# Modulation of a two-layer trunk: 32 of 48 column blocks as VectorE products with rows of the transposed weights

## The chip, the cores and the metric

The kernel runs on one core of one Trainium2 chip. A time is the device time of one execution in microseconds. The median of the runs of the kernel before is 5885.44 us (5885.08 to 5893.9, three runs). One further execution was profiled, and all rows come from it.

## The reference

A trunk of two layers works on 512 latent tokens x and 256 context tokens, 1024 wide, in float32. Each layer has a token mixer (four branches: pooling, a state space scan, a gated delta rule scan with a triangular inverse, a Fourier transform; each is weighted by gates and merged) and a retrieval of experts. Both are modulated: the shift, the scale and the gate of each of the two sub-layers are column blocks of one product of a conditioning vector with a matrix of 1024 x 6144.

```python
silu_c = jax.nn.silu(c)
silu_cc = jax.nn.silu(c_ctx)[None]
for l in range(DEPTH):
    mod_x = jnp.split(silu_c @ w_mod[l] + b_mod[l], 6, axis=-1)
    mod_c = jnp.split(silu_cc @ w_mod[l] + b_mod[l], 6, axis=-1)
    h_c = _modulate(ctx, mod_c[0], mod_c[1])
    if l == DEPTH - 1:
        states = context_states(h_c, lp, zero_states)
    else:
        mix_c, states = token_mixer(h_c, lp, zero_states, None)
        ctx = _layer_norm(DEEPNORM_ALPHA * ctx + mod_c[2][:, None] * mix_c, ...)
        ...
    h_x = _modulate(x, mod_x[0], mod_x[1])
    mix_x, _ = token_mixer(h_x, lp, states, rows)
    x = _layer_norm(DEEPNORM_ALPHA * x + mod_x[2][:, None] * mix_x, ...)
    ...
```

In the last layer the context is needed for the states of the scans alone, so only shift and scale (the first 16 column blocks of 128) of the context's modulation are used there; x uses all 48 blocks in both layers.

## The kernel before

`run` goes through the layers. A layer's mixer has two stages. In m1 the context is normalised and sent through the scans (`recurrent`); in m2 x goes through them, from the context's states. In layer 0's m2 the gather of experts for the context runs beside it: GpSimd gathers rows (`gat<-in_u`) and VectorE takes their dot products with a row `hb`, by a scalar_tensor_tensor of 128x1024 with an accumulated output (`gat<-gat,hb`).

A weight block is loaded as 128x512 in float32 (256 KB, tile `wraw`, or `xwraw` in the second lane, x), split into a high part (`xwhi`, ScalarE) and a low part (`xwlo`, VectorE), and multiplied on TensorE in three matmuls for each 128 columns. One unit of `gates` for the context takes four such loads, so 48 matmuls of 256 columns, then two tanh on ScalarE and two stores `gd<-xs` on SyncE's queue. A unit of gates for x has matmuls of 512 columns.

The modulation comes from `mod_steps`: for each of 12 groups of 512 columns, eight loads of 256 KB and eight matmuls with a result of 2x512 (both streams at once: x and context), a copy to SBUF, four small transposes and an addition of the bias into `modfm`. These matmuls take float32 operands as they are, and each shows as two instructions in the trace (`ps<-wraw,sc` in the first lane, `pa<-xwraw,sc` in the second). Layer 0's groups 0 to 3 (shift and scale of the first sub-layer) are made at the very start by `mod`, since the norm of the context waits for them. Groups 4 to 11 are the first filler of the second lane in layer 0's m1, ahead of the gates. All 12 groups of layer 1 are a filler added after layer 0's `mix_out`, with a low priority; in the scheduled program they stand in layer 0's m2, beside the scans of x and the gather.

Fillers are generators whose steps are called at points that a table (FC, FX) gives between the steps of the scans; over that a list scheduler decides the order of the instructions on each engine, once, when the program is built. Engines then work through their instructions in that order. DMA loads are issued by SyncE in such an order too. The tile `hb` (128x1024, `x4()`) has two buffers. The buffer `hx` holds the normalised x, transposed, in layer 0's m1.

All recorded instructions have the line of one helper, L145 (L155 in the kernel after).

## Time and profile before

| | us |
|---|---|
| median of three runs (lowest, highest) | 5885.44 (5885.08, 5893.9) |
| the profiled execution | 5897.45 |
| its span in the trace | 5895.7 |
| TensorE busy | 5041.2 (86%) |
| VectorE busy | 4232.6 (72%) |
| ScalarE busy | 1939.1 (33%) |
| GpSimd busy | 1862.3 (32%) |

The profile names engines PE (TensorE matmul), PEld (its weight loads), DVE (VectorE), ACT (ScalarE), POOL (GpSimd) and SP (SyncE, which issues loads and stores). Busy time of PE is a sum over pipelined matmuls, whose single durations overlap, so the pace of a row of matmuls is read from the starts. The chain of waits that the page gives covers the last part of the span alone, not the stages that the change touches; these are read by windows. The stages at hand are these: 0 to 66 us, the start up to the first four groups; 66 to 276, the context's projections and the modulation's other eight groups, up to the first row of the triangular inverse of the first stage; 276 to 545, the rest of the context's mixer; 1200 to 1420, layer 1's modulation in layer 0's m2; 3505 to 3663 and 3663 to 3800, layer 1's m1 before and after its inverse begins.

### The profile page before, as it was taken

The numbers are of one execution on the slowest core, as the hardware profiler recorded it, in microseconds if no ns is written. First come the engines' busy times: TensorE is split into PE (matmuls) and PEld (weight loads), VectorE is DVE, ScalarE is ACT, GpSimd is POOL, SyncE is SP. The second block draws the span as 40 slices with busy tenths as digits, with TensorE's granted clock in tenths as the row PEclk, the third lists the DMA queues.
The fourth block names the chain that finished last, engine by engine and source line by source line (L and its number), as shares of the span: only waits on it lengthen the run. The fifth ranks groups of instructions, "written<-read, shape, count | busy, mean of one in ns | idle before, by whom it ended". The sixth has DMA issues, their size and how long they took to land. (4 is left out here: it accounts for less than half of the span.)

```text
span 5895.7 us, 76828 instructions
## 1 busy us (share of the span) xinstructions
PE 5041.2 (86%) x26902; PEld 4234.5 (72%) x26902; DVE 4232.6 (72%) x7951; ACT 1939.1 (33%) x3519; POOL 1862.3 (32%) x1338
## 2 busy tenths in 40 slices
PE   8998977987568777799889879999888989988888
PEld 3887755843457677799667768787777989977766
DVE  4656287787888889788777786457565567877777
ACT  2444321321023322244323354333234323433333
POOL 0001544224553775544333310000003443433332
PEclk9999998998678888899999999999998989999999
DMA  6556469788887774999899954433434348998996
GB/s 214 177 164 194 143 227 312 245 259 315 275 278 266 241 245 150 315 350 346 315 326 345 328 197 136 124 113 111 135 125 133 126 142 282 350 331 325 327 335 242
DMA packets 613556, 1410.10 MB, mean 239 GB/s; under 512 B 97968, under 2 KB 221488, under 8 KB 613168
## 3 DMA queue, kind: packets, MB, share of 16 engines
q1 hardware_dynamic: 465712, 868.26, 43.8%
q0 software_dynamic: 147456, 536.94, 26.7%
q8 instruction: 211, 3.46, 0.2%
q14 instruction: 177, 1.45, 0.1%
HBM read 1244.52 MB, written 160.43 MB: 238 GB/s over the span
## 5 line engine op out<-in xcount | busy, mean ns | idle before, releaser
L145 POOL DMA_INDIRECT gat<-in_u,gidx x512 | 686.1, 1340 | 1038.2 <-DVE gat L145 959.9
L145 POOL DMA_INDIRECT gat<-in_v,gidx x512 | 651.3, 1272 | 906.1 <-DVE gacc L145 776.4
L145 DVE SCALAR_TENSOR_TENSOR gacc<-gat,gact,gacc 128x1024 f32<-128x1024 f32 x508 | 692.2, 1363 | 117.7 <-DMA gat<-in_v,gidx 112.8
L145 PE MATMUL ps<-hx 128*128 128x512 f32 x3072 | 752.7, 394 | 0.0
L145 DVE SCALAR_TENSOR_TENSOR gat<-gat,hb 128x1024 f32<-128x1024 f32 x512 | 617.6, 1219 | 108.5 <-DMA gat<-in_u,gidx 106.9
L145 PEld LDWEIGHTS ps<-hx 128*128 128x128 f32 x3072 | 588.5, 192 | 125.4
L145 PE MATMUL ps<-hx,dh 128*128 128x384 f32 x2304 | 601.8, 342 | 1.4 <-ACT dh L145 1.4
L145 PE MATMUL pa<-hx 128*128 128x512 f32 x1536 | 419.8, 408 | 170.7 <-ACT hx L145 157.8
L145 PE MATMUL ps<-s,s 128*128 128x128 f32 (+3 forms) x2752 | 420.3, 310 | 151.8 <-issue 83.9
L145 PEld LDWEIGHTS ps<-s,s 128*128 128x128 f32 (+1 forms) x2752 | 375.4, 213 | 225.3 <-issue 119.6
L145 ACT CAST dh<-du 128x1024 fp32r<-128x1024 f32 x256 | 268.6, 1051 | 785.5 <-PE ps L145 417.9
L145 PE MATMUL pa<-hx,dh 128*128 128x384 f32 x1792 | 511.3, 355 | 9.2 <-ACT da L145 7.4
L145 PEld LDWEIGHTS pa<-hx 128*128 128x128 f32 x1536 | 295.5, 196 | 248.9 <-ACT hx L145 164.6
L145 PEld LDWEIGHTS ps<-hx,dh 128*128 128x128 f32 x2304 | 422.0, 191 | 3.3 <-ACT dh L145 3.3
L145 PE MATMUL ps<-hx,dl 128*128 128x384 f32 x1152 | 393.3, 342 | 31.2 <-DVE dl L145 31.2
L145 PE MATMUL ps<-hx,whi 128*128 128x512 f32 x1152 | 386.9, 404 | 16.5 <-ACT whi L145 16.5
L145 DVE TENSOR_TENSOR hx<-dv,hx 128x1024 fp32r<-128x1024 f32 x256 | 313.0, 1223 | 119.0 <-ACT hx L145 115.1
L145 ACT CAST xwhi<-xwraw 128x512 fp32r<-128x512 f32 x352 | 218.2, 620 | 530.9 <-PE pa L145 418.8
L145 PE MATMUL pa<-hx,xwhi 128*128 128x512 f32 x1152 | 382.5, 406 | 8.0 <-DVE ld L145 3.6
L145 PE MATMUL pa<-hx,dl 128*128 128x384 f32 x896 | 322.8, 360 | 67.9 <-POOL dl L145 57.2
L145 ACT CAST hx<-dv 128x1024 fp32r<-128x1024 f32 x256 | 268.5, 1049 | 292.0 <-PE ps L145 175.7
L145 ACT CAST whi<-wraw 128x512 fp32r<-128x512 f32 x320 | 197.8, 620 | 490.6 <-PE ps L145 282.5
(283 smaller groups left out, 10177.9 us busy)
## 6 DMA issues: line engine op xcount, KB each, us to landing
du<-in_ut SPq DMA_DIRECT2D x256, 512.0 KB
dv<-in_v SPq DMA_DIRECT2D x256, 512.0 KB
xwraw<-in_w_in SPq DMA_DIRECT2D x272, 256.0 KB
acts<-da SPq DMA_DIRECT2D x256, 192.0 KB
a<-acts SPq DMA_DIRECT2D x256, 192.0 KB
wraw<-in_w_in SPq DMA_DIRECT2D x176, 256.0 KB
xwraw<-in_w_mod SPq DMA_DIRECT2D x160, 256.0 KB
rest<-wst SPq DMA_DIRECT2D x48, 768.0 KB
```

The source lines that it names most:

```text
L145: r = f(*a, **kw)
```

## The change

Groups 0 to 3 stay as they are. Column blocks 16 to 47 (groups 4 to 11) of both layers are computed by a new generator, `mod_rows`: for each block it loads 128 rows of the transposed weights (128x1024, 512 KB, into `hb`) and makes for each stream one scalar_tensor_tensor on VectorE, 128x1024, whose accumulated output is the dot product of each row with silu of the conditioning vector, which is broadcast over the partitions. The sum goes straight to its column of `modfm`. At the end the bias is added, once for all.

- Layer 0: both streams, so 64 products. They are no longer a filler of their own: `gates` for the context calls the generator twice after each of its 16 units (`beside`). The broadcast rows and the scratch output lie in three slices of the buffer that later becomes `hx`, so the norm of x (`norm_late`) allocates `hx` after that.
- Layer 1: x alone, 32 products, in layer 1's own m1, beside `gatesx`, with the row in the tile `gacc`. In layer 0's m2 four of the 12 groups stay.

```diff
+    def mod_rows(self, l, fm, streams, tiles):
+        nc, io = self.nc, self.io
+        n0 = 16
+        rows = []
+        for s in streams:
+            row = tiles[s]
+            nc.sync.dma_start(row, io["cr"][s:s + 1, :].to_broadcast([128, 1024]))
+            th = self.x4()
+            nc.scalar.activation(th, row, AF.Tanh, scale=0.5)
+            nc.vector.scalar_tensor_tensor(row, th, 1.0, row, op0=OP.add, op1=OP.mult)
+            rows.append(row)
+        for n in range(n0, 48):
+            w = self.x4()
+            nc.sync.dma_start(w, io["w_modt"][l, n - n0])
+            for i, s in enumerate(streams):
+                out = w if i == len(streams) - 1 else tiles[2]
+                nc.vector.scalar_tensor_tensor(out, w, 0.5, rows[i], op0=OP.mult, op1=OP.mult,
+                                               accum_out=fm[:, n, s:s + 1])
...
+            yield
...
-    def gates(self, l, h, T, gd, branches=range(4)):
+    def gates(self, l, h, T, gd, branches=range(4), beside=None):
...
                 self.proj_fm(self.io["w_in"][l], U_GATE + 4 * b + u, h, T, fn)
+                if beside is not None:
+                    for _ in range(2):
+                        next(beside, None)
                 yield
...
-                        self.add(self.mod_steps(l, range(4, 12), fm))
-                        gates = self.add(self.gates(l, hc, 256, mc[0]))
+                        free = [free[:, 1024 * i:1024 * i + 1024] for i in range(3)]
+                        gates = self.add(self.gates(l, hc, 256, mc[0], beside=self.mod_rows(l, fm, (0, 1), free)))
...
-                    gatesx = self.add(self.gates(l, hx, 512, mx[0], range(4 if last else 2)))
+                    self.add(self.norm_late(x, fm, hx))
+                    hx = hx.parts
+                    gatesx = self.add(self.gates(l, hx, 512, mx[0], range(4 if last else 2),
+                                                  self.mod_rows(l, fm, (0,), [self.keep([128, 1024], "gacc", 1)]) if last else None))
...
-                        self.add(self.mod_steps(l + 1, range(12), fm1))
+                        self.add(self.mod_steps(l + 1, range(4), fm1))
```

The order of instructions differs at three places. The first is VectorE in layer 0's m1, where the context's convolutions begin (`ps,vec` is a convolution's product, `wlo` and `xwlo` are low parts of split weights, `modfm` is the modulation). Before:

```order
L145 SCALAR_TENSOR_TENSOR s_221_622<-s_222_628,s_221_622 128x256
L145 SCALAR_TENSOR_TENSOR s_237_705<-ps_631,vec_6_75,s_237_705 128x254
L145 TENSOR_TENSOR wlo_782<-wraw_779,whi_781 128x512
L145 SCALAR_TENSOR_TENSOR s_237_705<-ps_631,vec_6_75,s_237_705 128x255 x2
L145 TENSOR_TENSOR wlo_820<-wraw_817,whi_819 128x512
L145 SCALAR_TENSOR_TENSOR s_237_705<-ps_631,vec_6_75,s_237_705 128x254
L145 TENSOR_TENSOR wlo_838<-wraw_835,whi_837 128x512
L145 SCALAR_TENSOR_TENSOR s_237_705<-s_238_711,s_237_705 128x256
L145 SCALAR_TENSOR_TENSOR s_239_714<-ps_632,vec_6_75,s_239_714 128x254
L145 TENSOR_TENSOR wlo_856<-wraw_853,whi_855 128x512
```

After (`hb` holds rows of the transposed weights, `hx` the broadcast rows and the scratch):

```order
L155 SCALAR_TENSOR_TENSOR hb_1282,modfm_179<-hb_1282,hx_131 128x1024
L155 SCALAR_TENSOR_TENSOR hx_131,modfm_179<-hb_1286,hx_131 128x1024
L155 TENSOR_TENSOR xwlo_1295<-xwraw_1292,xwhi_1294 128x512
L155 TENSOR_TENSOR wlo_698<-wraw_695,whi_697 128x512
L155 SCALAR_TENSOR_TENSOR hb_1286,modfm_179<-hb_1286,hx_131 128x1024
L155 TENSOR_TENSOR wlo_716<-wraw_713,whi_715 128x512
L155 TENSOR_TENSOR xwlo_1313<-xwraw_1310,xwhi_1312 128x512
L155 TENSOR_TENSOR wlo_754<-wraw_751,whi_753 128x512
L155 SCALAR_TENSOR_TENSOR hx_131,modfm_179<-hb_1370,hx_131 128x1024
L155 SCALAR_TENSOR_TENSOR s_235_731<-ps_657,vec_6_75,s_235_731 128x254
L155 TENSOR_TENSOR wlo_772<-wraw_769,whi_771 128x512
```

Products with the transposed rows, two to a load, and low parts of the gates' weights stand between the convolutions. Up to the inverse's first row VectorE has 27 `xwlo` splits before and 73 after, and all 64 products; all 16 gate units of the context stand ahead of the inverse, where 6 did. On SyncE's queue the 21 `xwraw` loads that lay among the first 32 `wraw` loads of the modulation at the start give way to 8 `xwraw` loads of the projection and two broadcast rows.

The second place is TensorE in layer 0's m2, at the state space scan of x (`s`, `masks`), with layer 1's modulation (`xwraw,sc`). Before:

```order
L145 MATMUL pa_15959<-xwraw_15963,sc_185 2x512
L145 MATMUL ps_11653<-s_2754_11651,s_2751_11644 128x256 x2
L145 MATMUL pa_15959<-xwraw_15966,sc_185 2x512
L145 MATMUL pa_15959<-xwraw_15969,sc_185 2x512
L145 MATMUL pa_15959<-xwraw_15972,sc_185 2x512
L145 MATMUL ps_11662<-s_2758_11660,masks_66 128x512
L145 MATMUL pa_15959<-xwraw_15975,sc_185 2x512
L145 MATMUL pa_15959<-xwraw_15978,sc_185 2x512
L145 MATMUL pa_15959<-xwraw_15981,sc_185 2x512
L145 MATMUL ps_11669<-s_2761_11667,masks_66 128x512
```

After, the last of the four groups that stay, and the scan behind it:

```order
L155 MATMUL ps_11128<-s_2588_11126,s_2585_11119 128x256 x2
L155 MATMUL pa_15699<-xwraw_15721,sc_185 2x512
L155 MATMUL ps_11137<-s_2592_11135,masks_66 128x512
L155 MATMUL pa_15726<-masks_66,xs_3804_15724 128x2 x4
L155 MATMUL ps_11144<-s_2595_11142,masks_66 128x512
L155 MATMUL ps_11153<-s_2599_11151,s_2585_11119 128x256 x2
L155 MATMUL ps_11162<-s_2603_11160,masks_66 128x512
L155 MATMUL ps_11169<-s_2606_11167,masks_66 128x512
L155 MATMUL ps_11174<-s_2587_11124,s_2594_11139 128x64
```

The eight later groups no longer stand between the scan's matmuls.

The third place is VectorE in layer 1's m1, at the context's convolutions. Before:

```order
L145 TENSOR_TENSOR xwlo_29880<-xwraw_29877,xwhi_29879 128x512
L145 SCALAR_TENSOR_TENSOR s_6235_29520<-s_6236_29526,s_6235_29520 128x256
L145 SCALAR_TENSOR_TENSOR s_6237_29529<-ps_29447,vec_8_80,s_6237_29529 128x254
L145 SCALAR_TENSOR_TENSOR s_6237_29529<-ps_29447,vec_8_80,s_6237_29529 128x255 x2
L145 SCALAR_TENSOR_TENSOR s_6237_29529<-ps_29447,vec_8_80,s_6237_29529 128x254
L145 TENSOR_TENSOR xwlo_29898<-xwraw_29895,xwhi_29897 128x512
L145 SCALAR_TENSOR_TENSOR s_6237_29529<-s_6238_29535,s_6237_29529 128x256
```

After:

```order
L155 SCALAR_TENSOR_TENSOR s_6084_29061<-ps_28979,vec_8_80,s_6084_29061 128x254
L155 SCALAR_TENSOR_TENSOR hb_30391,modfm_393<-hb_30391,gacc_27778 128x1024
L155 SCALAR_TENSOR_TENSOR s_6084_29061<-ps_28979,vec_8_80,s_6084_29061 128x255
L155 TENSOR_TENSOR wlo_29111<-wraw_29108,whi_29110 128x512
L155 SCALAR_TENSOR_TENSOR s_6084_29061<-ps_28979,vec_8_80,s_6084_29061 128x255
L155 TENSOR_TENSOR wlo_29129<-wraw_29126,whi_29128 128x512
L155 SCALAR_TENSOR_TENSOR s_6084_29061<-ps_28979,vec_8_80,s_6084_29061 128x254
L155 TENSOR_TENSOR xwlo_29759<-xwraw_29756,xwhi_29758 128x512
L155 SCALAR_TENSOR_TENSOR s_6084_29061<-s_6085_29067,s_6084_29061 128x256
L155 SCALAR_TENSOR_TENSOR s_6100_29144<-ps_29070,vec_8_80,s_6100_29144 128x254
L155 SCALAR_TENSOR_TENSOR hb_30548,modfm_393<-hb_30548,gacc_27778 128x1024
```

Products with x's row (`gacc`) stand between the convolution's steps, two to a gate unit. Up to the inverse's first row there are 32 `xwlo` splits where there were 24, so two gate units of 512 columns have moved ahead of it, and all 32 products stand there too. GpSimd's order is the same in both kernels.

## Rows read from the trace of the kernel before

**Rows 1.** The page, part 1: busy us (share of the span) xinstructions of each engine.

```profile
...
PE 5041.2 (86%) x26902; PEld 4234.5 (72%) x26902; DVE 4232.6 (72%) x7951; ACT 1939.1 (33%) x3519; POOL 1862.3 (32%) x1338
```

**Rows 2.** Windows: length, busy us of each engine, granted TensorE clock, DMA share, GB/s.

```profile
...
0.00:66.00 66.00, 51.10 (x129) 9.25 (x129) 7.49 (x23) 6.26 (x12) 1.29 (x6) 1.00 0.82 258
66.00:276.00 210.00, 196.41 (x1204) 146.54 (x1204) 135.34 (x285) 88.45 (x182) 3.76 (x2) 0.95 0.55 173
276.00:545.00 269.00, 238.36 (x1744) 220.00 (x1744) 165.07 (x336) 114.83 (x243) 7.09 (x6) 0.94 0.60 181
1000.00:1100.00 100.00, 94.36 (x409) 77.16 (x408) 89.19 (x159) 31.82 (x53) 41.46 (x35) 0.97 0.83 274
1305.00:1420.00 115.00, 100.07 (x334) 35.85 (x333) 88.05 (x158) 17.01 (x30) 49.77 (x41) 0.93 0.90 318
1420.00:1600.00 180.00, 90.93 (x457) 81.11 (x457) 139.28 (x232) 15.13 (x28) 92.64 (x78) 0.64 0.84 285
3505.00:3663.00 158.00, 148.06 (x859) 125.95 (x858) 104.45 (x214) 77.81 (x160) 4.93 (x4) 0.97 0.42 127
3663.00:3800.00 137.00, 133.83 (x725) 106.59 (x724) 68.87 (x158) 39.91 (x72) 0.00 (x0) 1.00 0.44 137
```

**Rows 3.** Waits of VectorE, 66 to 276 us: us in total, times, longest us.

```profile
...
DVE wlo L145 <- ACT whi L145: 18.9, 22, 3.7
DVE s L145 <- PE ps L145: 13.2, 12, 4.1
```

**Rows 4.** Groups of TensorE, 0 to 66 us: busy us, mean ns, idle before.

```profile
...
L145 PE MATMUL ps<-wraw,sc 128*2 128x512 f32 x64 | 33.3, 627 | 14.9 <-DMA wraw<-in_w_mod 14.6
L145 PE MATMUL pa<-xwraw,sc 128*2 128x512 f32 x40 | 20.3, 592 | 0.0
```

**Rows 5.** Timeline of TensorE near 131 us: start, length, instruction, count.

```profile
...
131.24 6.25 PE L145 MATMUL pa<-xwraw,sc 128*2 128x512 f32 x14
```

**Rows 6.** Groups of TensorE, 66 to 276 us.

```profile
...
L145 PE MATMUL pa<-xwraw,sc 128*2 128x512 f32 x88 | 41.9, 601 | 0.1
```

**Rows 7.** Timeline of VectorE: products with accumulate, back to back.

```profile
...
1296.21 1.22 DVE L145 SCALAR_TENSOR_TENSOR gat<-gat,hb 128x1024 f32<-128x1024 f32 x1
1297.36 0.08 DVE L145 DVE_READ_ACCUMULATOR gat<-gat,hb 128x1 f32 x1
...
1298.50 0.08 DVE L145 DVE_READ_ACCUMULATOR gat<-gat,hb 128x1 f32 x1
```

**Rows 8.** Timeline of SyncE: gate stores, two to a unit of 256 columns.

```profile
...
287.14 0.33 SPq L145 DMA_DIRECT2D gd<-xs  x1
...
293.07 0.33 SPq L145 DMA_DIRECT2D gd<-xs  x1
```

**Rows 9.** Groups of VectorE, 66 to 276 us.

```profile
...
L145 DVE TENSOR_TENSOR xwlo<-xwraw,xwhi 128x512 fp32r<-128x512 f32 x27 | 18.4, 687 | 10.2 <-ACT xwhi L145 9.1 <-DMA gd<-xs 1.2
```

**Rows 10.** Timeline of VectorE: first row of layer 0's first inverse.

```profile
...
276.12 2.11 DVE L145 TENSOR_TENSOR gat<-gat,gat 64x31 f32<-64x31 f32 x8 [1.81 <-DMA gat<-in_eye]
```

**Rows 11.** Waits of TensorE, 276 to 545 us.

```profile
...
PE pa L145 <- DVE ld L145: 13.1, 6, 5.9
```

**Rows 12.** Groups of TensorE, 1305 to 1420 us.

```profile
...
L145 PE MATMUL pa<-xwraw,sc 128*2 128x512 f32 x114 | 58.2, 628 | 9.8 <-DMA xwraw<-in_w_mod 9.8
...
L145 PE MATMUL pa<-masks,xs 2*128 2x2 f32 x32 | 3.4, 208 | 2.8 <-ACT xs L145 2.8
```

**Rows 13.** Waits of VectorE, 1305 to 1420 us.

```profile
...
DVE gat L145 <- DMA gat<-in_u,gidx: 9.7, 8, 2.4
```

**Rows 14.** Timeline of TensorE: matmuls of 512 columns.

```profile
...
3700.17 0.61 PE L145 MATMUL pa<-hx,xwhi 128*128 128x512 f32 x2
3700.63 0.39 PE L145 MATMUL pa<-hx,xwlo 128*128 128x512 f32 x1
```

**Rows 15.** Timeline of all engines: a 512 KB load and its reader.

```profile
...
596.10 1.53 SPq L145 DMA_DIRECT2D hb<-c  x2
...
600.52 0.69 DVE L145 BATCH_NORM_STATS2 bnst<-hb 128x6 f32<-128x512 f32 x1 [5.34 <-DMA hb<-c]
```

More of the change, by code (lines that the diff above doesn't have):

```diff
@@ L102, in __init__, with __getitem__ @@
         self.gen, self.pre, self.open, self.begun, self.at = gen, pre, [], False, 0
+class Late:
+    def __init__(self):
+        self.tile, self.parts = None, ([], [])
+    def __getitem__(self, at):
+        return self.tile[at]
 class Section:
@@ L488, in mod_steps @@
             yield
+    def mod_rows(self, l, fm, streams, tiles):
[16 more added lines that the diff above has]
+                                               accum_out=fm[:, n, s:s + 1])
+            if n == 47:
+                f = fm[:, n0:, :len(streams)]
+                b = self.vec[l][:, V_BM + n0:V_BM + 48]
+                nc.vector.tensor_tensor(f, f, b[:, :, None].to_broadcast([128, 48 - n0, len(streams)]), op=OP.add)
+                f = fm[:, 32:40, :len(streams)]
+                nc.vector.tensor_scalar(f, f, 1.0, None, op0=OP.add)
+            yield
     def bcast_row(self, fm, g, s, scale):
@@ L524, in parts, with norm_late @@
         return [hT[:, 0, k] for k in range(8)], [hT[:, 1, k] for k in range(8)]
+    def norm_late(self, x, fm, hx):
+        hx.tile = self.hx()
+        for a, b in zip(hx.parts, self.parts(hx.tile)):
+            a.extend(b)
+        yield from self.norm_steps(x, fm, 0, 0, hx.tile)
     def modulated(self, i, y, fm, g, s, hT):
@@ L1771, in run @@
             with ExitStack() as mix:
-                hx = self.hx()
+                free = None if last else self.hx(F32).rearrange("p a b c -> p (a b c)")
+                hx = Late()
                 mx = self.merged(512, hx)
@@ L1984, in layout @@
     out["w_sm"] = f(sm.reshape(L, 8, 128, 32).transpose(0, 2, 1, 3))
-    out["w_mod"] = f(a["w_mod"].reshape(L, 4, 2, 128, 12, 512).transpose(0, 4, 1, 3, 2, 5))
+    out["w_mod"] = f(a["w_mod"][:, :, :2048].reshape(L, 4, 2, 128, 4, 512).transpose(0, 4, 1, 3, 2, 5))
+    out["w_modt"] = f(a["w_mod"][:, :, 2048:].reshape(L, 1024, 32, 128).transpose(0, 2, 3, 1))
     wb = a["w_branch"]
@@ L2008, in layout @@
     out["ln"] = f(np.stack([a["ln1_g"], a["ln1_b"], a["ln2_g"], a["ln2_b"]], 1))
+    out["cr"] = f(np.stack([a["c"][0], a["c_ctx"]]))
     out["cc"] = f(np.stack([a["c"][0], a["c_ctx"]]).reshape(2, 8, 128).transpose(2, 0, 1))
```

2 lines of the change are left out of this document (removed).

## The prediction, as it was made before the result was known

> **What bounds the kernel now.** I read the totals first: TensorE is busy for 86% of the span, VectorE for 72% [rows 1]. On the averages the change is a trade from the fuller engine to the emptier one. But work is moved within three stretches only, so I read each by windows [rows 2]. Up to the first inverse (66 to 276 us) TensorE has 196 of 210 us and VectorE 135; VectorE's waits there are for ScalarE and for TensorE [rows 3], so TensorE sets the pace. From the inverse to the end of the context's mixer (276 to 545) TensorE has 238 of 269 us, and its largest wait is for VectorE's merges `ld` [rows 11]. In layer 1's m1 (3505 to 3663) it is 148 of 158, and after it 134 of 137. In layer 0's m2 (1305 to 1420) both are nearly full, 100 and 88 of 115. The chain of waits in the page covers the last sixth of the span, which the change does not touch.
>
> **Part A, layer 0's m1, start.** The start waits for weights: 64 instructions of the first four groups with 14.9 us of waits, 14.6 of them for loads [rows 4], at 258 GB/s [rows 2]. By the order, 21 loads of 256 KB that lie among them go, and 8 such loads and two broadcast rows come: about 2.4 MB less, 9 us at that rate. If TensorE set the end, the 40 instructions of the other lane there [rows 4] would give 40 x 0.43 = 17 us (14 in a row take 6.25 us, less the overlap 0.43 each [rows 5]). The loads are what it waits for, so I take 12, between 9 and 17: the stretch that began at 66 begins at 54.
>
> **Up to the inverse.** The remaining 88 modulation instructions there go, 41.9 us [rows 6], with 24 transposes of 0.11 [rows 12], 2.6 us. VectorE gets 64 products. The same form, 128x1024 with an accumulated result, is in the trace: back to back they start 1.145 us apart, the read of the accumulator included [rows 7]. That is 73.3 us, and two silu rows 2.4. What the diff does not show: the filler that stood ahead of the gates is gone, so the gates move up. By the order all 16 units stand ahead of the inverse, against 6; 46 splits more. One unit is four loads, and its stores are 5.93 us apart [rows 8], so 1.48 us of TensorE for each load, 68 us for 46; VectorE's splits are 0.687 each [rows 9], 31.6 us. TensorE then has 196.4 - 41.9 - 2.6 + 68 = 220 us, VectorE 135.3 + 73.3 + 2.4 + 31.6 - 1 (bias additions) = 242. **VectorE becomes the bound** of this stretch. How full can it be, in a stretch of convolutions and splits that wait for ScalarE [rows 3]? The window at 1000 us, with both engines loaded, has 89%; the one at 1420 us, with short dependent scan steps, 77.4%; 97.7% is the most that TensorE has in a window here [rows 2]. I take 89%, the row with the same two engines full: 272 us, so the inverse begins at 326 (276 before [rows 10]). With 97.7% it would be 302.
>
> **After the inverse.** The 46 loads' work is no longer there: TensorE 238.4 - 68 = 170 us. At the share of this window before, 0.886, it takes 192 us and ends at 518 instead of 545, a gain of 27. At the share of 66 to 276, 0.935, it would be 182; at 0.78, if chains that the gates filled lie open, 218. So A is worth 27, from 1 (218) up to the TensorE work that leaves: 128 x 0.43 + 32 x 0.11 = 58.
>
> **The loads of the products** come on SyncE's queue, in two buffers of `hb`, so the load for product k+2 waits for product k, and the weight loads behind it wait too. A load of this size lands 4.4 us after issue [rows 15] (with 1.53 us for two issues). In layer 0 a load serves two products, and 32 of them lie over 272 us, 8.5 us apart: I cost them at nothing, hidden by splits and convolutions. If the cover were gone, each would show up to 4.4 us.
>
> **Part B, layer 0's m2.** 8 of 12 groups leave, 114 instructions with 58.2 us busy and 9.8 us of load waits, and 32 transposes, 3.4 us [rows 12]. TensorE is left with 38 of 115 us. VectorE, less the bias additions, keeps 87, and gathers make it wait 9.7 [rows 13], which may shrink with 16.8 MB less on the DMA engines (0.90 busy [rows 2]). At 89% it takes 98 us, a gain of 17; at 77.4%, as in the next window with the same scan and gather and no modulation, 112, a gain of 3. I take 10, halfway, since both rows are near. The row after it has something else to say: with TensorE busy for 51% the granted clock is 0.64, against 0.93 here, so a mix of the two levels, 1.2 and 2.4 GHz [rows 2]. The Trainium skill, "TensorE: Matmul & The Clock Gate", Part 1: The HAM clock gate, says that an idle array is gated to half its clock and that activity releases the gate; this speaks against B. By that rule the 38 us at 0.93 become 55 at 0.64, 17 us more in a scan that waits for them, and B is 0 to 3: the sum would fall by 7.
>
> **Part C, layer 1's m1.** VectorE gets 32 products, 36.6 us, a silu row, 1.2, and by the order 8 more splits, 5.5: 104.5 + 43.3 = 148 of 158; at 89% 166. TensorE gets two gate units of 512 columns early, 8 loads x 12 matmuls x 0.23 us [rows 14] = 22: 148 + 22 = 170 at its share of 0.937, 181. TensorE still binds here, 23 us later, and after the inverse, where it has 97.7%, the 22 us come back. Here a load serves one product, 32 over 158 to 181 us with two buffers, 5 us apart against 4.4 us of landing: close. Waits of 10 to 14 us in all are likely, partly covered by TensorE's queue. I take a loss of 6 in all, between +5 (no waits, and merges after the inverse find more room) and -15 (all waits on the path, gates not paid back in full).
>
> **Sum.** 27 + 10 - 6 = 31 us. The profiled execution took 5897.45 us, 12 above the median of 5885.44, so it becomes 5866, and the median **5854**.
>
> **Rivals.** *Slower: VectorE cannot be kept full in the projections.* Convolutions, splits and products stand in one fixed order, and a split waits for ScalarE's high part. If layer 0's stretch has the 77.4% of the window at 1420 us, the inverse begins at 54 + 313 = 367, and with 192 us behind it ends at 559, 14 later. In layer 1 VectorE then needs 191 us, 33 more, of which 22 come back, and 5 of load waits: 16 later. B gives 3. Total -27: 5912. It decides at a share of 0.81, where the inverse begins at 353 and A is nought. For it: the waits in [rows 3], 89% is not reached in any projection of before; against it: there TensorE was the bound, so VectorE had to wait.
>
> *No change: what is freed does not reach the end.* The inverse, the scan's steps and the merges after it have a length of their own, and the gates were their filling; TensorE waits for `ld` already [rows 11]. With the 218 us above A gives 1, B 3, C -6: 5887. The lone `ld` waits of 13 us speak for it, the 0.886 share, with matmuls of merges and Fourier branch left as filling, against.
>
> *Products at half speed.* The trace has products of two float32 operands at 1.22 us [rows 7]. The Trainium skill, "Vector Engine (DVE) Microarchitecture Reference", section 7. Points that are easy to get wrong, says that this kind of instruction halves its throughput with two such operands from SBUF. If products were half as fast as in [rows 7], 1.15 us more each, A would lose 64 x 1.15 / 0.89 = 83, C some 25: 5962. The row is the same form, types and size, so whatever the rule counts from is already in 1.22 us.
>
> **How the numbers follow.** Forecast 0.60, no change 0.19, slower by VectorE's share 0.19, half speed 0.02. The forecast's own range is 5826 (A at 45, B at 17, C at -3) to 5873. The range for 8 in 10 adds the no-change case and stops at 5900, which leaves out most of the slower case (0.14), the half-speed case and 0.04 below. A difference of 0.2%, 12 us, is about what a measurement of this kernel can tell from no change: faster (below 5874) 0.60, same 0.19, slower (above 5897) 0.21.
>
> **What would show it.** The first product at 1.15 to 1.22 us; VectorE's share between the start's end (54) and the inverse's first row, 89% against 77%; that row at 326 (302 to 367); the end of the context's merges at 518; no waits of VectorE for `hb` in layer 0, some 10 us in layer 1; no modulation on TensorE after the four groups in m2, and the stretch of 1305 to 1420 shorter by 10, with the granted clock between 0.64 and 0.93. The forecast is wrong if VectorE waits for ScalarE or SyncE's loads between products, or if the inverse comes near 326 and the end does not follow.

## The result, and the profile after

The changed kernel is slower: 5921.68 us in the median of six runs against 5892.9 of the kernel before in the same number, ratio 1.0053 with an interval of 1.0038 to 1.0068, so about 31 us. The forecast was 5854, the range 5826 to 5900; both are missed, and the sign is the one of the rival.

The totals on the page of the kernel after answer [rows 1]: the profiled execution spans 5920.7 us, TensorE has 81 us less work, VectorE 105 us more.

```profile
...
PE 4960.0 (84%) x26582; PEld 4246.5 (72%) x26582; DVE 4337.1 (73%) x8130; ACT 1931.8 (33%) x3506; POOL 1874.0 (32%) x1338
...
```

The windows of the kernel after (columns as in [rows 2]), cut at its own landmarks:

```profile
...
0.00:60.00 60.00, 35.83 (x76) 4.71 (x76) 8.45 (x23) 5.81 (x11) 1.29 (x6) 0.97 0.74 232
60.00:338.00 278.00, 238.40 (x1703) 219.46 (x1702) 239.30 (x477) 128.26 (x266) 4.77 (x3) 0.93 0.65 205
338.00:553.00 215.00, 170.88 (x1152) 154.34 (x1152) 128.09 (x270) 75.49 (x162) 5.60 (x5) 0.90 0.51 154
1305.00:1420.00 115.00, 60.34 (x187) 36.91 (x186) 93.74 (x161) 11.83 (x21) 55.73 (x45) 0.62 0.67 213
1420.00:1600.00 180.00, 95.89 (x490) 86.20 (x490) 137.69 (x224) 17.22 (x30) 90.75 (x77) 0.68 0.84 286
3501.00:3688.00 187.00, 170.73 (x954) 144.94 (x955) 145.50 (x288) 86.45 (x173) 5.85 (x4) 0.96 0.67 214
3688.00:3918.00 230.00, 213.54 (x1044) 174.58 (x1042) 123.80 (x238) 71.37 (x125) 0.00 (x0) 0.93 0.34 102
...
```

And two windows of the kernel before with the ends that answer to these, from its inverse to the norm behind the context's mixer, and from layer 1's inverse to a step in its m2:

```profile
...
276.00:547.00 271.00, 239.87 (x1753) 221.07 (x1753) 166.06 (x338) 116.83 (x247) 7.09 (x6) 0.94 0.60 182
...
3663.00:3891.00 228.00, 224.83 (x1128) 183.35 (x1127) 128.26 (x246) 76.02 (x133) 0.19 (x1) 0.97 0.37 112
...
```

VectorE has 239 of 278 us up to the inverse, where it had 135 of 210; TensorE's clock in the stretch of layer 0's m2 fell from 0.93 to 0.62; in layer 1's m1 the stretch up to the inverse grew from 158 to 187 us, and the one behind it, with 11 us less of TensorE work, did not shrink (228 and 230).

The two traces hold the same instructions almost everywhere, so the difference is followed by the start of one instruction in both. The first row of layer 0's inverse ([rows 10] before) and the norm of the context behind its mixer, in VectorE's timeline of the kernel after:

```profile
...
338.18 2.75 DVE L155 TENSOR_TENSOR gat<-gat,gat 64x31 f32<-64x31 f32 x10
...
```

```profile
...
552.58 1.29 DVE L155 BATCH_NORM_STATS2 bnst<-hb 128x6 f32<-128x512 f32 x2 [1.04 <-DMA hb<-in_x]
...
```

The same norm in the kernel before:

```profile
...
547.23 1.28 DVE L145 BATCH_NORM_STATS2 bnst<-hb 128x6 f32<-128x512 f32 x2
...
```

Starts read in this way, in us, and lengths between them:

| | before | after | after less before |
|---|---|---|---|
| first row of layer 0's inverse | 276.12 | 338.18 | +62 |
| norm of the context behind the mixer | 547.23 | 552.58 | +5 |
| normalised queries and keys of x, layer 0's m2 | 1141.59 | 1141.71 | 0 |
| first accumulation of gathered rows | 1582.0 | 1571.59 | -10 |
| a norm at the start of layer 1's m1 | 3505.41 | 3501.17 | -4 |
| first row of its inverse | 3663.10 | 3688.06 | +25 |
| normalised queries and keys of x, layer 1's m2 | 3890.54 | 3918.14 | +28 |
| a norm behind layer 1's mixer | 4715.68 | 4743.68 | +28 |

So in these two traces part A made no gain but 5 us of loss, B gained 10, and C, from the norm at its start to the step in m2, lost 32 (385.1 to 417.0 us). Between these marks there is a drift that differs from one execution to the next, and a profiled execution lies up to 14 us from the median of its kernel's runs, so the times of the runs, not the marks, decide on totals; the marks tell where. Over all traces of this document, A's loss at the context's norm is 6 us (mean 554.8 in six traces with the whole of layer 0's part, from 550.4 to 559.5; 549.1 in five with layer 0 as before, from 546.3 to 552.5), and at the queries and keys of x in layer 0's m2 it is 2. B's stretch, from these queries and keys to the first accumulation, is 440.4 in the trace of before, but 434.1 to 441.7 in the seven traces with 12 groups there, 437.8 in the mean.

### The profile page after: what moved, and what is told of

The parts are those of the page before. It is cut to its first block, busy times and chain, and to the rows that moved or that the text cites. A ratio compares the mean times of both kernels' runs of the same rounds, so it can differ in the third digit from the quotient of the medians.

```text
span 5920.7 us, 76244 instructions
## 1 busy us (share of the span) xinstructions
PE 4960.0 (84%) x26582; PEld 4246.5 (72%) x26582; DVE 4337.1 (73%) x8130; ACT 1931.8 (33%) x3506; POOL 1874.0 (32%) x1338
## 5 line engine op out<-in xcount | busy, mean ns | idle before, releaser
L155 PE MATMUL ps<-s,s 128*128 128x128 f32 (+3 forms) x2752 | 448.5, 324 | 218.7 <-DVE s L155 106.7
L155 PEld LDWEIGHTS ps<-s,s 128*128 128x128 f32 (+1 forms) x2752 | 399.1, 225 | 290.4 <-issue 162.4
```

The source lines that it names most:

```text
L155: r = f(*a, **kw)
```

## The experiments

Each ratio is that of the kernel against the kernel before, run in turn on the same chip, with its interval; that of a kernel before to after was 1.0053. Diffs show the lines that matter, with `...` for what is left out, against the changed kernel or the kernel that the text names; where a run has more than four groups of a layer as matmuls, the array of their weights is laid out as before.

### Each layer's part alone

**l0_only** keeps layer 0's part and goes back to matmuls in layer 1:

```diff
-                                                  self.mod_rows(l, fm, (0,), [self.keep([128, 1024], "gacc", 1)]) if last else None))
+                                                  None))
...
-                        self.add(self.mod_steps(l + 1, range(4), fm1))
+                        self.add(self.mod_steps(l + 1, range(12), fm1))
...
```

> Layer 0's part of the change alone: its eight groups become 64 products beside the gates; layer 1 keeps its 12 groups as matmuls in layer 0's m2. The prediction's sum gives 27 us less than before. A reading of the two traces has the loss elsewhere: the first inverse row at about 338 us (276 before), the end of the context's mixer some 5 us later than before, and nothing left of that by 1229 us; this theory expects the time of before within 6 us. If layer 0 is the cause of the slowdown after all, some 25 us more than before.

**l1_only** keeps layer 1's part and goes back to matmuls in layer 0, with the norm of x and its buffer `hx` as before too:

```diff
-                        gates = self.add(self.gates(l, hc, 256, mc[0], beside=self.mod_rows(l, fm, (0, 1), free)))
+                        self.add(self.mod_steps(l, range(4, 12), fm))
+                        gates = self.add(self.gates(l, hc, 256, mc[0]))
...
```

> Layer 1's part alone: four of its groups stay in layer 0's m2, 32 products go into its own m1; layer 0 keeps its eight groups as matmuls. The prediction's sum gives 10 less in layer 0's m2 and 6 more in layer 1's m1, so 4 us less than before. The traces' reading has 10 less and 31 to 33 more, so some 20 to 25 us more than before, the whole slowdown.

Measured: l0_only 1.0022 (1.0012 to 1.0032), some 13 us more; l1_only 1.0040 (1.0025 to 1.0055), some 24 more. Both parts lose, and together they make the 31 us of the whole within the intervals. The reading of the traces had layer 0's part at nothing, which the runs do not bear out. The marks agree with those of the whole change: in l0_only the inverse begins at 341.55 and the context's norm at 557.39, 10 us late; in l1_only the stretch of m1 to m2 takes 416.3 us, 31 more than before. At the queries and keys of x l0_only's trace is only 2.5 us behind that of before, and this execution took 5895.36 us, where the median is 5903.05, so where the rest of its 13 us lies is not shown.

### What layer 0's modulation costs in either form

**l0_none** leaves the eight groups of layer 0 out of l0_only; `mod_bias` copies the bias into their columns:

```diff
-beside=self.mod_rows(l, fm, (0, 1), free)
+beside=self.mod_bias(l, fm, (0, 1))
```

> Layer 0's eight groups are left out: no matmuls, no products, no loads for them, only the bias stands in these columns; layer 1 is as before. It asks what the freed TensorE time is worth with no VectorE work in its place. If the stretch is bound by work, all of the 58 us of TensorE work that leave show, 40 to 58 us less than before. If the chain from the inverse to the end of the merges limits, as in the rival of no change, 10 us less or nothing.

**l0_narrow** keeps l0_only's loads, and lets each product read 64 columns:

```diff
-                nc.vector.scalar_tensor_tensor(out, w, 0.5, rows[i], op0=OP.mult, op1=OP.mult,
+                nc.vector.scalar_tensor_tensor(out[:, :64], w[:, :64], 0.5, rows[i][:, :64], op0=OP.mult, op1=OP.mult,
```

> Layer 0's part alone, but each of its 64 products reads 64 of 1024 columns, with all loads kept. Leaving products and loads out altogether put the end of the context's mixer 54 us earlier than with them. If VectorE's time is the price there, this comes within 12 us of that kernel, some 0.7 to 0.9% under the kernel before; if the loads on SyncE's queue are, it stays near the kernel with whole products, 0 to 0.3% above the kernel before. In that one VectorE waited for these loads for 0.7 us in all, which speaks for its time.

Measured: l0_none 0.9913 (0.9900 to 0.9927), 51 us under the kernel before; l0_narrow 0.9952 (0.9933 to 0.9970), 28 under. The first is the outcome expected if work bounds the stretch; the second lies between the two that were expected. The windows up to the inverse and from it to the norm behind the mixer, of l0_none, l0_narrow and l0_only:

```profile
...
60.00:275.00 215.00, 201.17 (x1482) 187.09 (x1481) 151.56 (x309) 108.32 (x223) 3.76 (x2) 0.95 0.53 162
275.00:503.00 228.00, 197.57 (x1376) 178.93 (x1375) 144.61 (x306) 93.72 (x204) 6.63 (x6) 0.92 0.56 169
...
```

```profile
...
60.00:286.00 226.00, 206.30 (x1511) 191.51 (x1510) 164.64 (x443) 112.75 (x230) 3.76 (x2) 0.95 0.71 232
286.00:515.00 229.00, 194.21 (x1348) 175.18 (x1346) 142.59 (x304) 90.83 (x198) 6.72 (x6) 0.91 0.55 164
...
```

```profile
...
60.00:342.00 282.00, 243.42 (x1702) 223.63 (x1702) 240.30 (x479) 127.52 (x265) 4.78 (x3) 0.91 0.65 202
342.00:557.00 215.00, 171.94 (x1152) 154.89 (x1152) 127.30 (x266) 75.84 (x163) 5.61 (x5) 0.90 0.51 153
...
```

The norm begins at 502.58, 514.68 and 557.39, and at 547.23 in the kernel before. So at this mark the matmuls with their loads cost 45 us; the products cost 55, of which the loads are 12 and VectorE's time 43. The runs put the loads at 23 us, give or take 13, and VectorE's time at 41, so the split is known within some ten us only. Most of TensorE's 58 us of work was indeed on the path, as the prediction had it, and could be won back. But 73 us of VectorE took more than that in its place. VectorE waited for a load of the products for 0.6 us in all up to the inverse (kernel after, groups of VectorE):

```profile
...
L155 DVE TENSOR_TENSOR xwlo<-xwraw,xwhi 128x512 fp32r<-128x512 f32 x73 | 49.1, 683 | 3.7 <-ACT xwhi L155 3.1 <-DMA gd<-xs 0.6
L155 DVE SCALAR_TENSOR_TENSOR hx<-hb,hx 128x1024 f32<-128x1024 f32 x34 | 41.2, 1215 | 0.8 <-DMA hb<-in_w_modt 0.6 <-ACT hb L155 0.2
L155 DVE SCALAR_TENSOR_TENSOR hb<-hb,hx 128x1024 f32<-128x1024 f32 x32 | 38.9, 1217 | 0.0
...
```

The second windows show the other half. TensorE has 198, 194 and 172 us of work behind the inverse, and the stretch takes 228, 229 and 215 (240 of 271 before). From before to l0_none 42 us of work less gave 43 us; from l0_none to l0_only 26 us less gave 13, and the share fell from 0.87 to 0.80. TensorE's wait for the scan's own steps on VectorE (`s`), in the kernel before (276 to 547 us) and after (338 to 553):

```profile
...
PE ps L145 <- DVE s L145: 5.2, 3, 4.4
...
```

```profile
...
PE ps L155 <- DVE s L155: 19.2, 11, 6.1
...
```

In l0_none it is 4.1 us, in l0_only 19.3. TensorE is idle for 31, 30, 44 and 43 us of these stretches (before, l0_none, after, l0_only), so the growth of this one wait (14 us) is as large as that of the idle time (13): with the gates gone, the scan's steps lie open.

### Where the products stand, and how many

**l0_own** makes l0_only's products a filler of their own ahead of the gates (`four_rows` yields after each fourth block):

```diff
-                        gates = self.add(self.gates(l, hc, 256, mc[0], beside=self.mod_rows(l, fm, (0, 1), free)))
+                        self.add(self.four_rows(self.mod_rows(l, fm, (0, 1), free)))
+                        gates = self.add(self.gates(l, hc, 256, mc[0]))
```

> Layer 0's part alone, but its products form a filler of their own ahead of the gates, four blocks to a step, where the matmuls stood; by the order 47 splits of gate weights stand ahead of the inverse, where the changed kernel has 76 and the one before 27. VectorE's work ahead of the inverse falls by 20 us, so the inverse begins some 22 us earlier, at about 318. If work that lies behind the inverse takes its full time, the end of the context's mixer stays where it was, since the gates come back there (within 5 us of the layer 0 part alone). If the stretch behind the inverse is bound by its chain at some 195 us, most of the 22 us are gained.

Measured: 1.0035 (1.0025 to 1.0046), 8 us over l0_only, with intervals that overlap. The inverse did not come 22 us earlier (341.69), though VectorE had 25 us less to do ahead of it, and the norm came at 583.13, so neither expected outcome is met. The profiled execution took 5927.37 us, where the median is 5913.27, so the trace shows more of a loss than the runs.

```profile
...
60.00:342.00 282.00, 207.52 (x1348) 185.66 (x1348) 215.15 (x429) 101.38 (x207) 3.76 (x2) 0.81 0.55 169
342.00:583.00 241.00, 209.86 (x1505) 192.38 (x1504) 152.81 (x317) 101.93 (x218) 6.30 (x6) 0.94 0.58 175
...
```

TensorE's waits up to the inverse, in l0_own (us in total, times, longest us):

```profile
...
PE ps L155 <- DVE s L155: 21.7, 6, 6.2
PE pa L155 <- DVE xwlo L155: 19.2, 8, 9.7
PE ps L155 <- ACT s L155: 12.9, 3, 11.6
...
```

With products in a row and fewer gates between, TensorE waits for VectorE for 41 us in the two groups, with a share of 0.74 and a granted clock of 0.81. So the share of VectorE, 0.76 here, is set by the order, and this is the rival's 77%, though in this kernel and not in the changed one. The gates pulled ahead, which the prediction counted as a burden on the inverse, seem to be what kept TensorE fed; TensorE had 36 us less to do here than in l0_only, in the same 282 us.

**half_tick1** makes half of layer 0's groups products (32); layer 1's products are in its m2 as in l1_tick1 below. `gates` still calls the generator twice after each unit, so the products are not one block to a gate unit, as was meant: all stand beside the first eight units, and the last is done at 197 us:

```diff
...
+                        self.add(self.mod_steps(l, range(4, 8), fm))
-                        gates = self.add(self.gates(l, hc, 256, mc[0], beside=self.mod_rows(l, fm, (0, 1), free)))
+                        gates = self.add(self.gates(l, hc, 256, mc[0], beside=self.mod_rows(l, fm, (0, 1), free, 32)))
```

> Layer 0 with half of the change: groups 4 to 7 stay matmuls ahead of the gates, groups 8 to 11 become 32 products, one block to a gate unit; layer 1's products spread over its m2, one to a step, which by itself came out level with the kernel before. If a product's price rises with VectorE's load ahead of the inverse, half of the products cost under half: 5 to 20 us below the kernel before. If price is the same for each, about level, within 6 us. If products and matmuls add up on the path, 10 us above.

Measured: 1.0039 (1.0027 to 1.0051). That is 23 us above the kernel before, where 10 were expected if matmuls and products add up. The inverse begins at 319.82, the norm at 563.54, 16 later than before and 61 later than in l0_none; half of the 45 and half of the 55 us above would be 50. So half of the products do not cost less than half, and both forms together cost more than their halves. Whether half of the products would do so spread over all 16 units was not tried.

```profile
...
60.00:320.00 260.00, 234.51 (x1643) 205.18 (x1640) 196.77 (x394) 121.09 (x248) 3.82 (x2) 0.96 0.65 206
320.00:564.00 244.00, 189.01 (x1256) 171.12 (x1256) 137.06 (x294) 84.40 (x186) 6.46 (x6) 0.87 0.47 143
...
```

VectorE has only 0.76 of the first window; TensorE has 0.90 of it and 0.77 of the second. In the second stretch, 244 us with 189 us of work at a clock of 0.87, TensorE waits 19.5 us for the scan's steps `s` on VectorE, as after the whole change, and 14 more for split weights (9.3 for `xwhi`, 4.5 for `xwlo`); why these came late was not followed.

### Low parts on GpSimd

**pool0** is l0_only with the low parts of the context's gate weights on GpSimd; **before_pool0** is the same edit in the kernel before, the control:

```diff
+                self.lo_pool = l == 0 and T == 256
                 self.proj_fm(self.io["w_in"][l], U_GATE + 4 * b + u, h, T, fn)
+                self.lo_pool = False
```

> Layer 0's part alone, with the low parts of the context's gate weights (64 of them) computed on GpSimd, which has 9 us of work in that stretch; one takes 1.32 us there (0.69 on VectorE), 84 us in all. If VectorE's time ahead of the inverse is what the change pays with, this takes some 40 us off it: the inverse at about 300 to 315, and 20 to 35 us less than the layer 0 part alone, so below the kernel before. If GpSimd slows VectorE when both work, or SyncE's queue is the limit, less than 10.

> The control: the kernel before with the same 64 low parts on GpSimd. TensorE is the bound there by the profile, so it should gain little: within 6 us of the kernel before, or a loss if a low part that takes twice as long delays TensorE.

Measured: pool0 1.0032 (1.0019 to 1.0044), before_pool0 1.0037 (1.0025 to 1.0050): no gain over l0_only (1.0022), and a loss in the control. In pool0 the inverse begins at 363.55, 22 us later than in l0_only. Groups up to 340 us, of VectorE and of GpSimd:

```profile
...
L155 DVE SCALAR_TENSOR_TENSOR hx<-hb,hx 128x1024 f32<-128x1024 f32 x34 | 51.8, 1527 | 2.0 <-DMA hb<-in_w_modt 1.8 <-ACT hb L155 0.2
L155 DVE SCALAR_TENSOR_TENSOR hb<-hb,hx 128x1024 f32<-128x1024 f32 x32 | 51.1, 1596 | 0.1
...
```

```profile
...
L155 POOL TENSOR_TENSOR xwlo<-xwraw,xwhi 128x512 fp32r<-128x512 f32 x61 | 103.6, 1715 | 157.0 <-ACT xwhi L155 123.6 <-DMA wraw<-in_w_in 19.5 <-PE pa L155 13.1
...
```

The same products take 1527 and 1596 ns, where they took 1215 and 1217, and a low part takes 1715 ns on GpSimd, where one took 1399 in before_pool0. The 44 us that left VectorE (64 x 0.687) were given back by what stayed on it: up to the inverse it is busy for 254 us, where l0_only has 240. The products make 23 us of that; much of the rest is in other operations on SBUF tiles, as `s<-s,s` of 128x512, which takes 1060 ns where it took 691.

### Layer 1's m1: VectorE's time or the loads

**l1_none** is the changed kernel without layer 1's products and loads, **l1_narrow** has all loads and products of 64 columns, **l1_noload** whole products on two loads. The edits, in this order:

```diff
-self.mod_rows(l, fm, (0,), [self.keep([128, 1024], "gacc", 1)]) if last else None
+self.mod_bias(l, fm, (0,)) if last else None
...
+                c = 64 if l == L - 1 else 1024
-                nc.vector.scalar_tensor_tensor(out, w, 0.5, rows[i], op0=OP.mult, op1=OP.mult,
+                nc.vector.scalar_tensor_tensor(out[:, :c], w[:, :c], 0.5, rows[i][:, :c], op0=OP.mult, op1=OP.mult,
...
-            w = self.x4()
-            nc.sync.dma_start(w, io["w_modt"][l, n - n0])
+            if l < L - 1 or n % 16 == 0:
+                w = self.x4()
+                nc.sync.dma_start(w, io["w_modt"][l, n - n0])
```

> As the changed kernel, but layer 1's products and their loads are left out, only the bias stands in those columns. Layer 0's part is as in the changed kernel. If the products (their VectorE time and their loads) make the 31 us that layer 1's m1 lost, the time is that of before less 10 for layer 0's m2, some 31 to 38 us under the changed kernel. If the loss came from elsewhere in that stage (a changed order, the clock), it stays within 10 us of the changed kernel.

> As the changed kernel, but each of layer 1's 32 products reads 64 of its 1024 columns, with all loads of 512 KB kept: the VectorE time of the products falls from 37 us to some 4, the loads stay on SyncE's queue. The kernel without products and loads left some 22 us under the changed one. If VectorE's time is the cause, this gains 18 to 25 us on the changed kernel; if the loads (their place on the queue, the two buffers, the weight loads behind them) are the cause, it gains under 6.

> As the changed kernel, but layer 1's 32 products take their rows from two loads, each used 16 times, where 32 were made: VectorE's work is whole, 30 loads of 512 KB are left out, and the products' results are not the modulation. If VectorE's time is the cause, this stays within 6 us of the changed kernel; if the loads are, it gains 18 to 25 us.

Measured: 1.0010 (1.0001 to 1.0019), 1.0047 (1.0030 to 1.0064) and 1.0039 (1.0026 to 1.0053). l1_none wins back 25 of the 31 us, less than the 31 to 38 expected; the other two are within their intervals of the whole change, so neither theory alone fits. The marks in these traces tell more. From the norm at the start to the inverse, and from there to the step in m2:

| | to the inverse | behind it | sum |
|---|---|---|---|
| before | 157.7 | 227.4 | 385.1 |
| after | 186.9 | 230.1 | 417.0 |
| l1_none | 159.0 | 228.6 | 387.5 |
| l1_narrow | 174.7 | 231.8 | 406.5 |
| l1_noload | 175.7 | 225.1 | 400.8 |
| l1_qgpsimd | 202.7 | 222.4 | 425.1 |

The loads without VectorE's time cost 19 us over l1_none, VectorE's time without the loads 13, both together 30. Nine traces without these products have sums of 383.6 to 389.5, so each of the two is on the path, and within this spread they add up. The runs alone could not tell that: they put the loads at 22 us over l1_none and VectorE's time at 17, each give or take some ten, and both together at 25. The windows of l1_none and l1_noload:

```profile
...
3510.00:3669.00 159.00, 148.42 (x858) 127.36 (x858) 104.14 (x213) 77.53 (x160) 4.94 (x4) 0.96 0.41 126
3669.00:3898.00 229.00, 224.61 (x1128) 182.56 (x1127) 128.34 (x246) 76.19 (x133) 0.18 (x1) 0.97 0.36 112
...
```

```profile
...
3511.00:3687.00 176.00, 165.67 (x943) 142.39 (x943) 144.06 (x287) 83.25 (x171) 5.46 (x4) 0.97 0.43 135
3687.00:3912.00 225.00, 211.74 (x1054) 172.25 (x1052) 124.29 (x239) 72.95 (x128) 0.00 (x0) 0.95 0.35 107
...
```

In l1_noload TensorE has 17 us more to do ahead of the inverse, gates that moved up, and 13 less behind it, but that stretch gets only 3 to 4 us shorter, its share falling from 0.98 to 0.94. What stands open there is seen in the matmuls of the inverse and of the scan (`ps<-s,s`), in the kernel before (3663 to 3891 us) and after (3688 to 3918), busy time, mean and idle time before them:

```profile
...
L145 PE MATMUL ps<-s,s 128*128 128x128 f32 (+1 forms) x272 | 32.4, 266 | 2.3 <-DVE s L145 1.3 <-issue 1.0
...
```

```profile
...
L155 PE MATMUL ps<-s,s 128*128 128x128 f32 (+1 forms) x272 | 39.9, 306 | 13.0 <-issue 5.6 <-DVE s L155 5.2 <-ACT s L155 2.2
...
```

The same 272 matmuls take 7 us more, at a granted clock of 0.93 where it was 0.97, and TensorE idles 11 us more before them. The stretch has 11 us less work in spite of these 7, so some 19 us of gates left it, and 18 were taken up here.

**l1_qgpsimd** has the loads issued by GpSimd:

```diff
-            nc.sync.dma_start(w, io["w_modt"][l, n - n0])
+            (nc.gpsimd if l == L - 1 else nc.sync).dma_start(w, io["w_modt"][l, n - n0])
```

> As the changed kernel, but layer 1's 32 loads of 512 KB are issued by GpSimd, which has 6 us of work in that stage, where SyncE issued them; buffers, bytes and products are the same. Layer 1's m1 lost 30 us with the change, 23 with narrow products and all loads, 15 with whole products and two loads. If the loads cost because SyncE waits for their buffers and the weight loads queue behind it, this gains 10 to 18 us on the changed kernel. If they cost because two buffers or the DMA engines' time limit them, under 6.

Measured: 1.0069 (1.0048 to 1.0090), an interval that overlaps that of the changed kernel, and in that stage 38 us over l1_none, where the changed kernel has 30. So taking the loads off SyncE's queue does not make them cheaper. The run is no pure test of the queue, since the profile lists GpSimd's loads under a queue of another kind (software_dynamic, where SyncE's is hardware_dynamic). DMA issues up to the inverse, their count, size and median us to landing, in l1_none, l1_narrow and l1_qgpsimd:

```profile
...
wraw<-in_w_in SPq DMA_DIRECT2D x35, 256.0 KB, 2.9
xwraw<-in_w_in SPq DMA_DIRECT2D x20, 256.0 KB, 3.1
...
```

```profile
...
hb<-in_w_modt SPq DMA_DIRECT2D x32, 512.0 KB, 5.8
wraw<-in_w_in SPq DMA_DIRECT2D x34, 256.0 KB, 3.3
xwraw<-in_w_in SPq DMA_DIRECT2D x22, 256.0 KB, 4.4
...
```

```profile
...
hb<-in_w_modt POOLq DMA_DIRECT2D x32, 512.0 KB, 4.7
wraw<-in_w_in SPq DMA_DIRECT2D x37, 256.0 KB, 3.7
xwraw<-in_w_in SPq DMA_DIRECT2D x28, 256.0 KB, 4.4
...
```

Weight loads land after 2.9 and 3.1 us without the products' loads, after 3.3 and 4.4 or 3.7 and 4.4 with them. ScalarE's wait for weights in the first lane, up to the inverse, in the kernel before, in l1_narrow, in the kernel after and in l1_qgpsimd:

```profile
...
ACT whi L145 <- DMA wraw<-in_w_in: 14.9, 18, 2.6
...
```

```profile
...
ACT whi L155 <- DMA wraw<-in_w_in: 18.6, 15, 3.4
...
```

```profile
...
ACT whi L155 <- DMA wraw<-in_w_in: 27.9, 18, 4.3
...
```

```profile
...
ACT whi L155 <- DMA wraw<-in_w_in: 40.9, 19, 4.6
...
```

It is 15, 19, 28 and 41 us, and 16 in l1_none. Twice the bytes are on the DMA engines (40.0 MB up to the inverse, 214 GB/s, where l1_none has 20.1 MB and 126 GB/s), and each weight load lands later. But this is a part of the loads' price only: TensorE's own wait for these high parts is 5.2 us before, 6.2 in l1_none, 9.1 in l1_narrow, 9.7 in the kernel after and 19.3 in l1_qgpsimd. So late weights can answer for the 8 us between the last two, and for some 3 of the 19 us that l1_narrow has over l1_none. The rest of the 19 was not followed; TensorE is idle for 27 us of the two stretches in l1_narrow, where it is for 15 in l1_none. In the kernel after SyncE waits 32.6 us for `hb` (3497 to 3690 us); that this held the products' loads back and so spared the weights is a reading, not shown. More buffers for `hb` were not tried.

### Layer 1's products in its m2

**l1_tick2** and **l1_tick1** keep layer 0 as before, and put layer 1's products behind the steps of its m2, two or one to a step; **tick1_q** is the latter with loads issued by GpSimd. The line for one to a step (it is 2 in l1_tick2):

```diff
+                    if last:
+                        self.ticking(self.mod_rows(l, fm, (0,), [self.keep([128, 1024], "gacc", 1)]), 1)
...
```

> Layer 0 as before; layer 1's 32 products moved out of its m1 into its m2, where x is scanned, two behind each of the steps at which layer 0 gathers, tied to these steps. In that stretch VectorE is busy for about half of the time and TensorE for 96%, so VectorE has room. If a product costs only where VectorE is close to full, this is 8 to 12 us below before (what the four remaining groups leave free in layer 0's m2). If products delay TensorE's feed wherever they stand, it is 15 to 30 above.

> As the one with two products to a step, but with one, so that they are spread over twice the stretch. If products cost by crowding, this is 0 to 5 us better than with two; if the place does not matter, the same.

> Layer 0 as before, layer 1's products spread over its m2, one to a step, and their loads issued by GpSimd. With SyncE's queue this came out level with the kernel before. If its loss of some 4 to 8 us in that stage came from SyncE's queue, this is 5 to 12 us below the kernel before (the gain in layer 0's m2 alone is 3 to 10); else level.

Measured: 1.0006 (0.9993 to 1.0018), 0.9997 (0.9984 to 1.0009) and 1.0015 (1.0001 to 1.0030). m1 is whole again: 387.7, 389.5 and 384.8 us between the two marks. From there to the norm behind the mixer it is 835.8, 829.0 and 834.8 us, where before has 825.1, so 32 products cost 11 us there crowded, 4 spread, 10 with GpSimd's queue. That spreading pays is not shown: half_tick1 has the same products at the same steps as l1_tick1, and 834.5 us, and the intervals of l1_tick2 and l1_tick1 overlap. Among 13 traces without products in this stretch, 12 have 823 to 828 us and one (pool0) 833.6. GpSimd's queue brought no gain either. B's gain is of the same size: 6, 7 and 5 us between its marks against the trace of before. No version that does the whole work beat the kernel before; l1_tick1 equals it.

## Why the prediction was wrong, step by step

**The start** was to gain 12 us. The last transposes of the first groups end at 61 where they ended at 66: 5. The step took the loads' bytes and TensorE's work, but 22 us of load waits stayed where 14.6 were counted [rows 4]: with less work between, TensorE only waited longer. Mis-sized by 7.

**Up to the inverse** the sum held for VectorE. It has 239 us of work (242 forecast), a product 1.215 us at 1.145 from start to start, VectorE's share 0.86 (0.89 forecast), or 0.90 if the 11 us of the start's last wait are taken out. The inverse began 62 us late, where 50 was forecast: 7 of the 12 are the start. TensorE has 238 us, where 220 were forecast (five loads of the merges' weights, `xwraw<-in_w_branch`, came ahead too), so both engines have a share of 0.86. That VectorE's time is on the path there is shown by l0_narrow, whose inverse begins at 285.94 where l0_only has 341.55.

**Behind the inverse** is the step that failed for layer 0. TensorE's 170 us of work were right (171), but the share of 0.886 was not: 0.80, so 214 us where 192 were forecast [rows 2]. The stretch, read to the norm, got shorter by 57 us, where 269 - 192 = 77 were forecast: 20 less. A share read with the gates as filling was used for a stretch without them. l0_none shows the limit: with 198 us of work the share is still 0.87, and the next 26 us of work give only 13. This is the mechanism of the rival of no change, which had 218 us there, and TensorE's wait for the scan's steps (19.2 us, where 5.2 before) shows it. 27 - 7 - 5 - 20 = -5: as measured in the marks of these two traces. By the runs of l0_only the loss is 13, from 7 to 19.

**Part B** was 10, and is 10 in this trace; over ten traces that have four groups there it is 2 to 13 between the marks against this trace of before, 7 in the mean, against the 3 to 17 forecast; against the mean of the seven traces with 12 groups (437.8) it is 4. The granted clock fell to 0.62 in the stretch with TensorE at 52% of it (60 us, where the prediction had 55 at a clock of 0.64), and to 0.56 and 0.57 in l1_none and l1_only, nearer to the level of 1.2 GHz. The rule of the Trainium skill, "TensorE: Matmul & The Clock Gate", Part 1: The HAM clock gate, that an array left idle is gated, agrees with these rows. The row at 0.64 [rows 2] was at hand, and the better estimate would have leaned to the lower end. VectorE is at 82% there. The 10 of the one trace is partly luck.

**Part C** was -6 and is -32. Two steps failed. The first: "the 22 us come back". TensorE does have 23 us more ahead of the inverse (171 us where it had 148), and the stretch behind it had 11 less, but it takes as long as before, at a share of 0.93 where it had 0.99. This is the same error as in layer 0, with the opposite share: 97.7% busy [rows 2] was read as work that sets the time; once work left, the matmuls of the inverse and the scan took 7 us more and left TensorE idle 11 us more. Over the two windows of the stage TensorE is idle for 13 us before and 33 after, and busy for 373 and 384. The second: the loads, of whose 10 to 14 us of VectorE's waits 5 were put on the path. The waits were 9.8 us, about as forecast; but by the marks of l1_narrow the loads cost 19 us by themselves, with hardly any VectorE time. That they make other loads late, and TensorE wait for weights, is some 3 us of that; where the rest comes from stays open.

**The rivals.** The slower case gave 5912 by a VectorE share of 0.77 ahead of the inverse. The sign and nearly the size are right, the mechanism is not: the share was 0.86. The time went where the no-change rival had it, behind the inverse, and in layer 1 to the products' loads, which no rival priced at that. *Products at half speed* is refuted: 1.215 us in place, for two float32 operands from SBUF, as in [rows 7].

## What to carry to other kernels

Work that is pulled ahead of a serial chain need not come back behind it: here 57 of 77 us came back in layer 0, and none of 22 in layer 1. The share of an engine in a stretch holds only for the work that fills it now, so ask what the stretch takes with its filling gone. An engine with a quarter of its time idle on average is not free: moving 58 us of TensorE work into 73 us of VectorE work in the same stage cost some 13 us by the runs, and the leave-out run (51 us faster) is the cheap way to learn what there is to win before the work is placed anew. Loads for moved work can cost more than the waits of their own reader; look at who else has loads in flight there. And before a difference of a few us between two marks is read as a price, see how far the same stretch differs among traces of kernels that are alike in it.

## What the hardware showed beside that

GpSimd and VectorE slowed each other: in pool0, with low parts on GpSimd at the same time, VectorE's products of 128x1024 took 1527 and 1596 ns where they took 1215 and 1217, and GpSimd's subtraction of 128x512 went from 1399 ns (before_pool0, without the products) to 1715 ns. VectorE's operations that read their operand from PSUM (the convolutions' products of 128x254) did not change, 476 ns against 477. And loads made other loads land later: 256 KB weight loads went from about 3.0 us (l1_none) to between 3.3 and 4.4 us (l1_narrow, l1_qgpsimd) when 512 KB loads ran beside them.
